# Attention scores in a two-block transformer kernel: the low part of the queries on 128 rows instead of 64

## Chip, cores and metric

One core of a Trainium2 chip. The metric is the device time of one execution in microseconds (us), median of the runs.

## What is computed

Two transformer layers (the first with retention, the second with neighbourhood attention over a grid of 512 latent tokens and 256 context tokens) and then one block with causal attention of 20 heads, a recurrent branch and gates. The change touches the two attentions, whose scores are products of queries and keys of 64 features per head. First the scores of layer 1 (16 heads, one row of the grid at a time, qr scaled by 1/8), then those of block 2 (12 dilated-window heads and 8 block heads over 512 tokens):

```
s_lat = jnp.einsum('bnqhd,brnkhd->bhnqrk', qr, kb).astype(jnp.float32) + bias[None].astype(jnp.float32)
s_lat = jnp.where(col_ok[:, :, None, :], s_lat, NEG_INF).reshape(B, NA_HEADS, n_cb, NA_QBLOCK_W, wr * NA_BAND_W)
s_ctx = jnp.einsum('bnqhd,bchd->bhnqc', qr, kc).astype(jnp.float32)
p = jax.nn.softmax(jnp.concatenate([s_lat, s_ctx], -1), -1).astype(v.dtype)
...
logits = jnp.einsum('bdhnqe,bdhnke->bdhnqk', qb, kk).astype(jnp.float32) * SCALE
logits = logits + bias[None, None, :, None]
...
lg = jnp.einsum('bhnqe,bhnke->bhnqk', qb, kb).astype(f32) * SCALE + bias_own[None, :, None]
```

## The kernel before, in words

All matrix products work on fp32r operands that are split in two: a rounded high part and the remainder, the low part, so that a product is high x high + high x low + low x high. ScalarE (ACT) writes the high part with a copy, VectorE (DVE) subtracts it from the source for the low part. Weights are loaded as slabs of 128 x 1024 (`Stream`, 384), split likewise, and live with nearly everything else in one pool of 86 tiles of 128 x 512 (`S`, 453).

The program is recorded first and then issued in the order of a list schedule (`Recorder.plan`, 152, and `issue`, 312): priority is program order, each instruction has a cost by its shape, and an instruction goes early if its engine is free and its tiles are. All instructions therefore carry line 321 in the profile, and are told apart by their tiles.

A pair of heads shares a projection. `na_proj` (1241, layer 1, 8 pairs) and `b2_proj` (1524, block 2, 10 pairs) multiply a weight slab with the activations (matmuls `bank<-act,w`), which leaves 128 x 512 in PSUM, head A on rows 0 to 63 and head B on rows 64 to 127. `q_stack` (1230) makes the queries: ACT copies each head's high part twice, onto both halves of a tile `qh` of its own; DVE subtracts once per head, and both low parts share one tile `ql`, A on rows 0 to 63, B on 64 to 127. `k_stack` (1237) makes a tile `kt` per head with the high part of the keys on one half of the rows and the low part on the other (`kc` for the context keys). So one matmul over 128 rows gives q high x (k high + k low), and a second over 64 rows adds q low x k high. Both are in `qk_mm` (1284), and follow each other in the same PSUM bank:

```
PE.matmul(out, H["q"][:, q0:q0 + 128], kt[:, c0:c1], start=True, stop=False)
PE.matmul(out, H["ql"][o:o + 64, q0:q0 + 128], kt[o:o + 64, c0:c1], start=False, stop=True)
```

In the profile the first is `bank<-kt,qh` or `bank<-kc,qh`, the second `bank<-kt,ql` or `bank<-kc,ql`. The queries are the stationary operand (128 columns), the keys the moving one (128, 256, 384 or 512 columns).

A head of layer 1 (`na_attn`, 1387) has 8 such pairs of matmuls (`na_scores`, 1301); DVE takes the maximum (tiles `mx`) and adds the bias (`s`), ACT takes exponentials, DVE divides (`na_soft`, 1325), PE transposes with the identity (`bank<-ident,sc`, `bank<-ident,s`), ACT and DVE split the result into high and low (`pt`, `na_trans`, 1340), PE multiplies with the values (`bank<-pt,vc`, `bank<-pt,vt`, `na_out`, 1370). The attention of pair p is interleaved with the projection of pair p + 1 (`interleave`, 426). A head of block 2 has 4 pairs (`Soft.scores`, in the class at 1548); `a_attn` (1633) takes three heads together, `c_attn` (1655) one at a time, again interleaved with projections. In the trace the first attention lies from 1384 to about 1672 us, the second from 2164 to about 2400.

Of the kernel before, what the change touches and what calls it, by code (L numbers as in the profile page):

```python
# [49 lines left out]


class Recorder:
    """Collects the program in program order, then issues it in the order of a list schedule.

    Priority is program order; a tile is taken ahead of program order only while every earlier
    instruction still finds its tiles free.
    """
    WINDOW = 2500
    SPARE, NEAR = 16, 200

# [89 lines left out]
        return n / (1.92 if fast else 0.96) + 69 + 60 * ptr, 0  # L150

    def plan(self):
        """List schedule of the program: its length, and when each instruction starts and ends."""
        ops = self.ops
        N = len(ops)
        prio = [op[7] for op in ops]
# [55 lines left out]
        while nd < N:  # L212
# [12 lines left out]
            while progressed:  # L225
                progressed = False
                for e in engs:
# [19 lines left out]
                    i = held  # L247
# [107 lines left out]


class Slab:
    """A [128, 1024] weight slab kept as two tiles."""

    def __init__(self, pool):  # L360
        self.t = [pool.tile([128, 512], F32R, name="w", tag="s", bufs=NSLOT) for _ in range(2)]
# [87 lines left out]
def body(nc, tc, io, sp, wp, pp, dp, order, stop=None, dbg=None):  # L449
# [3 lines left out]
    def S(dt=F32, name="s"):  # L453
        return sp.tile([128, 512], dt, name=name, tag="s", bufs=NSLOT)
# [71 lines left out]
            DVE.scalar_tensor_tensor(out if it == 2 else y, t, 1.5, y, op0=ALU.add, op1=ALU.mult)  # L526

    def mm3(out, a, b, start, stop):
        """a, b: (hi, lo) pairs of access patterns; a is stationary."""
        PE.matmul(out, a[0], b[0], start=start, stop=False)  # L530
        PE.matmul(out, a[0], b[1], start=False, stop=False)
        PE.matmul(out, a[1], b[0], start=False, stop=stop)

    # ---------------------------------------------------------------- constants
    kp = sp
    ident = kp.tile([128, 128], F32, name="ident", tag="ident", bufs=1)
    NCOL = io["cols"].shape[1] if order is not None else 1
# [19 lines left out]
    cond_bc = {}  # L557

    def ada_block(l, chunk, j, parts):
        """Shift or scale of features 128 j and up: products with the condition, summed along k on DVE."""  # L560
        for p in range(parts):
            if p not in cond_bc:
                cond_bc[p] = [S(name="cbc") for _ in range(2)]
                for g in range(2):
                    src = io["c_rows"][p:p + 1, g * 512:g * 512 + 512]
                    nc.sync.dma_start(cond_bc[p][g], src.to_broadcast([128, 512]))
                    ACT.activation(cond_bc[p][g], cond_bc[p][g], AF.Silu)
        w = [S(name="aw") for _ in range(2)]
        for g in range(2):
            nc.sync.dma_start(w[g], io["w_ada_t"][ADA_T.index((l, chunk)) * 8 + j][:, g * 512:g * 512 + 512])  # L570
        for p in range(parts):
            m = mcol[l][chunk][p][:, j:j + 1]
            for g in range(2):
                out = w[g] if p == parts - 1 else S(name="aj")
                init = m if g else col("ada_b", l * 48 + chunk * 8 + j)
                DVE.tensor_tensor_reduce(out, w[g], cond_bc[p][g], 1.0, init, ALU.mult, ALU.add, accum_out=m)

    def ada_pe(j):
        """Shift of layer 0, features 128 j and up, on PE."""
        b = bank()  # L580
        for k in range(8):
            if k % 4 == 0:
                w = S(name="ak")
                nc.sync.dma_start(w, io["w_ada_k"][j][:, k * 128:k * 128 + 512])
            PE.matmul(b[0:2, 0:128], cond[:, 2 * k:2 * k + 2], w[:, k % 4 * 128:k % 4 * 128 + 128],
                      start=(k == 0), stop=(k == 7))
        rows = S(name="rows")
        ACT.activation(rows[0:2, 0:128], b[0:2, 0:128], AF.Copy)
        PE.transpose(b[:, 256:258], rows[0:2, 0:128], ident[0:2, 0:2])
        for p in range(2):  # L590
            DVE.tensor_tensor(mcol[0][0][p][:, j:j + 1], b[:, 256 + p:257 + p], col("ada_b", j), op=ALU.add)
# [6 lines left out]
        ada_done.add((l, chunk))  # L598

    def ada_gate(l, chunk, parts):  # L600
        """A gate, token rows times features: sums over the partitions by ones on PE."""
        acc = {(p, g): None for p in range(parts) for g in range(2)}
        for g in range(2):
            for k in range(8):
# [27 lines left out]
    def ada_bg(l, chunk, parts):  # L632
        return (ada_gate if chunk in (2, 5) else ada_cols)(l, chunk, parts)

    # ------------------------------------------------------------ weights / GEMMs
    def out_banks(parts):
        return {p: bank() for p in parts}

    def t_mm(banks, w, act, ks, kts, cut=None, wk0=0):
        """T-form: out[128 features, tokens]; weights stationary."""  # L640
        h, l = w
        for k in ks:
            wa = (h[:, (k - wk0) * 128:(k - wk0) * 128 + 128], l[:, (k - wk0) * 128:(k - wk0) * 128 + 128])
            for pi, (wi, xi) in enumerate(((0, 0), (0, 1), (1, 0))):
                for p, b in banks.items():
                    c0, c1 = (0, 256 if p == "c" else 512) if cut is None else cut
                    PE.matmul(b[:, c0:c1], wa[wi], act.ap(k, xi, p, c0, c1),
                              start=(k == kts[0] and pi == 0), stop=(k == kts[-1] and pi == 2))
# [5 lines left out]
        return banks  # L654

    def t_gemm_first(keys, act, segs):
        """First slabs of a GEMM whose input arrives segment by segment."""
        wts = [ws.get(*k) for k in keys]
        parts = []
        for s in segs:  # L660
            if s[0] not in parts:
                parts.append(s[0])
        banks = [out_banks(parts) for _ in keys]
        for part, c0, c1, pre in segs:
            if pre is not None:
                pre()
            for b, w in zip(banks, wts):
                t_mm({part: b[part]}, w, act, range(8), range(8), (c0, c1))
                tick()
        return banks  # L670
# [4 lines left out]

    def r_sweep(name, base, nslab, act, tiles, k0=0, tail=0, on_tile=None, banks=None, fill=None, first=0,
                pre=None, width=512):
        """Row form: out[tokens, width]; activations stationary, 1024 // width k-tiles a slab."""
        banks = [bank() for _ in tiles] if banks is None else banks
        kps = 1024 // width  # L680

# [31 lines left out]
            ws.done(tail)  # L713
        return banks

    # ------------------------------------------------------------------ LN parts
    def add_gated(R, i, half, b, gate):
        if gate is None:
            DVE.tensor_tensor(R[i][half], b, R[i][half], op=ALU.add)
# [39 lines left out]
        return ap.rearrange("p (r n c) -> p n r c", r=8, n=4)  # L759

    def blocks(ap):
        """Grid columns of a [128, 512] tile kept column block by column block."""
        return ap.rearrange("p (n r c) -> p n r c", n=4, r=8)

    def to_T(rows, part, c0, act, G, Bc, grid=False):
        """rows: two token tiles (halves); writes act columns c0..c0+256 of `part`."""
        for kb in range(4):
            b = bank()
            for kk in range(2):
# [58 lines left out]
    TL0 = [("c", 0), ("c", 128)] + [("l", 128 * i) for i in range(4)]  # L828
    TL1 = [("l", 128 * i) for i in range(4)]

    # ================================================================= layer 0
    for ch in (2, 3, 4, 5):
        background.append(ada_bg(0, ch, 2))
    aT = Acts()
# [248 lines left out]
            ACT.activation(R[i][half], R[i][half], AF.Copy, scale=ALPHA)  # L1083

    def bound(sweep0, sweep1, R, tiles, gates, chain, segs_T, early=True):
        """Two half sweeps into rows; returns the hooks that finish the transposition.

        gates[i] is the gate of tile i; chain(i) runs once tile i is summed; segs_T(pair) transposes.
        """
        n = len(tiles)  # L1090
        banks = sweep0()
        for i in range(n):
# [110 lines left out]
    del uT, fT  # L1203
    dump("xn1", R[2][0])

    # ================================================================= layer 1
    ga, ba = bcast_row(io["ln_g"][1:2], ALPHA), bcast_row(io["ln_b"][1:2], ALPHA)
    h0d = dp.tile([512, 1024], F32, name="h0d", tag="h0d")

# [17 lines left out]

    HT = {}

    def q_stack(ps, scale, qa, qb, ql):  # L1230
        for q, p0 in ((qa, 0), (qb, 64)):
            for o in (0, 64):
                ACT.activation(q[o:o + 64], ps[p0:p0 + 64], AF.Copy, scale=scale)
            DVE.scalar_tensor_tensor(ql[p0:p0 + 64], ps[p0:p0 + 64], scale, q[p0:p0 + 64], op0=ALU.mult,
                                     op1=ALU.subtract)

    def k_stack(ps, p0, kt):
        ACT.activation(kt[p0:p0 + 64], ps[p0:p0 + 64], AF.Copy)
# [2 lines left out]
    def na_proj(p):  # L1241
# [4 lines left out]
            yield  # L1246
        A, B = {"o": 0}, {"o": 64}
        HT[2 * p], HT[2 * p + 1] = A, B
        A["q"], B["q"], ql = S(F32R, "qh"), S(F32R, "qh"), S(F32R, "ql")
        A["ql"] = B["ql"] = ql  # L1250
        q_stack(b["l"], 0.125, A["q"], B["q"], ql)
        ws.done()
        raw, rawc = S(name="vr"), S(name="vr")
        nc.sync.dma_start(raw.rearrange("p (t c) -> p t c", t=4),
# [27 lines left out]
        yield  # L1282

    def qk_mm(out, H, q0, kt, c0, c1):
        o = H["o"]
        PE.matmul(out, H["q"][:, q0:q0 + 128], kt[:, c0:c1], start=True, stop=False)
        PE.matmul(out, H["ql"][o:o + 64, q0:q0 + 128], kt[o:o + 64, c0:c1], start=False, stop=True)

    KB = ((0, 2), (0, 3), (1, 4), (2, 4))

# [164 lines left out]
    X = {}  # L1455

    def chain_h(i):
        """h = LN(z) rows, kept for the residual; X = h / rms(h)."""
        mv, rstd = ln_rstd(i)
        for half in range(2):  # L1460
            DVE.scalar_tensor_tensor(R[i][half], R[i][half], mv[:, 0:1], ga[half], op0=ALU.subtract, op1=ALU.mult)
# [13 lines left out]
    del uT, fT  # L1475
    dump("h1", R[0][0])

    # ================================================================= block 2
    h1d = dp.tile([4, 2, 128, 512], F32, name="h1d", tag="h1d")
    for i in range(4):  # L1480
        for half in range(2):
# [42 lines left out]
    def b2_proj(qn, kn, t, heads):  # L1524
# [4 lines left out]
            yield  # L1529
        A, B = {"o": 0}, {"o": 64}  # L1530
        HT[heads[0]], HT[heads[1]] = A, B
        A["q"], B["q"], ql = S(F32R, "qh"), S(F32R, "qh"), S(F32R, "ql")
        A["ql"] = B["ql"] = ql
        q_stack(b["l"], 0.125, A["q"], B["q"], ql)
        ws.done()
        w = ws.get(kn, t)
        b = out_banks("l")
# [8 lines left out]
        yield  # L1546

    class Soft:
        """Causal attention of one output head over one or more groups of keys."""

        def __init__(self, heads, st):
            self.heads, self.st = heads, st
# [122 lines left out]
    def chain(*gs):  # L1675
        for g in gs:
            yield from g
# [345 lines left out]
```

## Time and profile before

| what | value |
|---|---|
| median of 3 runs | 3029.85 us |
| lowest and highest | 3027.33 and 3034.6 us |
| profiled execution, span from first to last instruction | 3022.2 us |
| its own time with what lies around the span | not listed; the median is 7.65 us above the span |
| granted TensorE clock, mean over the span | 0.981 of 2.4 GHz |
| busy share PE, DVE, ACT, POOL | 97%, 54%, 37%, 23% |

The page gives shares over the whole span, the views of the trace give single stretches. Matmuls are pipelined: the next starts before the one ahead ends, so the duration of one is longer than its place in the queue, and a row of the timeline with xN runs from the first start to the last end. PEld is the load of a stationary tile.

### The profile page before, as it was taken

Reading aid. Unit: us, or ns where it says so; the run is one execution under the profiler, and the core shown is the slowest. Engines: PE = TensorE matmul, PEld = TensorE weight load, DVE = VectorE, ACT = ScalarE, POOL = GpSimd, SP = SyncE. Lnnn points to the kernel's source line nnn. Section 1 sums busy time; section 2 is a strip of 40 time slices with the busy share of each in tenths; the row PEclk is TensorE's granted clock in tenths of the full one; section 3 lists DMA queues with packets and bytes.
Section 4 is the critical chain, followed back from the end, with each engine's and each line's share of the span. In section 5 each row is a group of like instructions: output and inputs, shape, how many; then the busy total and the mean of one; then the engine's idle time right before and its main releaser. Section 6 shows DMA issues by size and latency. Waiting matters only on the chain.

```text
span 3022.2 us, 37734 instructions
## 1 busy us (share of the span) xinstructions
PE 2943.5 (97%) x13988; PEld 2418.1 (80%) x13988; DVE 1640.3 (54%) x3351; ACT 1105.1 (37%) x2343; POOL 706.0 (23%) x592
## 2 busy tenths in 40 slices
PE   7999999998999999999999899998999999999998
PEld 5788888887888888877777788886777778888887
DVE  8887544428735344554777932337365673553233
ACT  4332333512221222224656432323465653332231
POOL 4311213106212112251221521104333201121100
PEclk9999999999999999998999999998999999999999
DMA  8333212322324333231212332334422222332231
GB/s 312 112 129 108 91 51 82 119 94 87 117 75 163 102 108 133 89 130 56 70 63 84 106 105 70 100 110 155 149 84 84 70 84 91 119 102 80 77 112 42
DMA packets 120462, 311.01 MB, mean 103 GB/s; under 512 B 12646, under 2 KB 22230, under 8 KB 120278
## 3 DMA queue, kind: packets, MB, share of 16 engines
q1 hardware_dynamic: 120278, 308.60, 31.0%
q8 instruction: 110, 1.80, 0.2%
q14 instruction: 74, 0.61, 0.1%
HBM read 292.77 MB, written 22.33 MB: 104 GB/s over the span
## 4 chain that ended last, share of the span: by engine, by line
PE 90%; DVE 6%; DMA 2%; ACT 1%; issue 1%; POOL 1%; SPq 0%; DVEq 0%; ACTq 0%; POOLq 0%
PE bank L321 90%; DVE rs_t L321 1%; DVE R L321 1%; DVE w L321 1%; DVE rs_g L321 1%; DVE act L321 1%; DMA ak<-w_ada_k 0%; DMA xl<-xT 0%; DVE bn L321 0%; DVE gt L321 0%; DMA aw<-w_ada 0%; DVE rstd L321 0%; ACT w L321 0%; DMA cbc<-c_rows 0%; DVE X L321 0%
## 5 line engine op out<-in xcount | busy, mean ns | idle before, releaser
L321 PE MATMUL bank<-act,w 128*128 128x512 f32 (+1 forms) x6960 | 1452.6, 367 | 11.3 <-ACT act L321 6.5
L321 PEld LDWEIGHTS bank<-act,w 128*128 128x128 f32 x6960 | 1186.6, 191 | 233.0 <-issue 9.6
L321 DVE TENSOR_TENSOR w<-raw,w 128x512 fp32r<-128x512 f32 x664 | 524.2, 812 | 546.0 <-PE bank L321 333.0
L321 ACT ACTIVATE w<-raw 128x512 fp32r<-128x512 f32 x748 | 440.2, 628 | 516.9 <-PE bank L321 362.9
L321 PE MATMUL bank<-w,act 128*128 128x512 f32 (+1 forms) x1728 | 391.8, 387 | 4.3 <-DVE w L321 3.3
L321 PEld LDWEIGHTS bank<-w,act 128*128 128x128 f32 x1728 | 320.1, 190 | 70.4 <-DVE w L321 4.4
L321 PE MATMUL bank<-w,f 128*128 128x512 f32 x1584 | 365.0, 390 | 0.0
L321 PEld LDWEIGHTS bank<-w,f 128*128 128x128 f32 x1584 | 297.4, 188 | 61.4
L321 POOL TENSOR_TENSOR f<-sg,f 128x512 fp32r<-128x512 f32 x66 | 86.7, 1313 | 520.3 <-ACT f L321 505.5
L321 POOL TENSOR_TENSOR R<-gt,R 128x512 f32<-128x512 f32 x64 | 88.1, 1397 | 383.5 <-DVE gt L321 369.7
L321 POOL TENSOR_TENSOR w<-raw,w 128x512 fp32r<-128x512 f32 x84 | 111.1, 1349 | 203.7 <-ACT w L321 180.3
L321 PE MATMUL bank<-w,yT 128*128 128x512 f32 x576 | 133.5, 393 | 0.0
L321 PEld LDWEIGHTS bank<-w,yT 128*128 128x128 f32 x576 | 108.6, 189 | 22.5
L321 ACT ACTIVATE f<-sg 128x512 fp32r<-128x512 f32 x66 | 41.7, 632 | 202.0 <-DVE sg L321 201.9
L321 ACT ACTIVATE pt<-bank 128x384 fp32r<-128x384 f32 (+3 forms) x176 | 72.7, 470 | 100.9 <-PE bank L321 100.2
L321 DVE TENSOR_TENSOR pt<-bank,pt 128x384 fp32r<-128x384 f32 (+3 forms) x176 | 84.4, 522 | 45.7 <-ACT pt L321 42.7
L321 DVE TENSOR_TENSOR sg<-bank,sg 128x512 f32<-128x512 f32 x66 | 45.4, 688 | 109.1 <-PE bank L321 109.1
L321 POOL TENSOR_TENSOR act<-tt,act 128x256 fp32r<-128x256 f32 (+1 forms) x88 | 77.5, 908 | 80.2 <-DVE act L321 71.7
L321 ACT ACTIVATE s<-s,nm 128x384 f32<-128x384 f32 (+3 forms) x144 | 79.5, 559 | 35.4 <-DVE nm L321 35.4
L321 POOL TENSOR_TENSOR R<-R,bc 128x512 f32<-128x512 f32 x56 | 81.2, 1464 | 15.2 <-PE bank L321 13.4
L321 DVE TENSOR_TENSOR gt<-bank,gbc 128x512 f32<-128x512 f32 x64 | 42.9, 685 | 76.4 <-PE bank L321 71.5
L321 DVE SCALAR_TENSOR_TENSOR acc<-aw,cond,acc 128x512 f32<-128x512 f32 x84 | 67.6, 830 | 27.0 <-DMA aw<-w_ada 26.4
(217 smaller groups left out, 3079.4 us busy)
## 6 DMA issues: line engine op xcount, KB each, us to landing
raw<-w_w SPq DMA_DIRECT2D x132, 512.0 KB, 3.5
aw<-w_ada_t SPq DMA_DIRECT2D x112, 256.0 KB, 4.4
raw<-w_b_gu SPq DMA_DIRECT2D x44, 512.0 KB, 3.5
aw<-w_ada SPq DMA_DIRECT2D x64, 256.0 KB, 5.1
raw<-w_b_gt SPq DMA_DIRECT2D x24, 512.0 KB, 3.5
raw<-w_b_dn SPq DMA_DIRECT2D x22, 512.0 KB, 3.6
raw<-w_ret_qk SPq DMA_DIRECT2D x16, 512.0 KB, 3.5
raw<-w_ret_v SPq DMA_DIRECT2D x16, 512.0 KB, 4.7
```

What stands on the lines that cost most here:

```text
L321: ins = fn(*a, **k).ins
```

## The change

`q_stack` now makes a `qh` and a `ql` of its own for each head, and writes the low part onto both halves of the tile, with two subtractions per head where there was one. `qk_mm` multiplies the whole 128 rows of `ql` with the whole 128 rows of `kt`, so that the second matmul also has 128 rows; it now adds q low x (k high + k low). The low x low part was not computed before. A few texts between triple quotes and comments are gone too.

```
-    def q_stack(ps, scale, qa, qb, ql):
-        for q, p0 in ((qa, 0), (qb, 64)):
+    def q_stack(ps, scale, A, B):
+
+        for H, p0 in ((A, 0), (B, 64)):
+            q, ql = H["q"], H["ql"] = S(F32R, "qh"), S(F32R, "ql")
             for o in (0, 64):
                 ACT.activation(q[o:o + 64], ps[p0:p0 + 64], AF.Copy, scale=scale)
-            DVE.scalar_tensor_tensor(ql[p0:p0 + 64], ps[p0:p0 + 64], scale, q[p0:p0 + 64], op0=ALU.mult,
-                                     op1=ALU.subtract)
+            for o in (0, 64):
+                DVE.scalar_tensor_tensor(ql[o:o + 64], ps[p0:p0 + 64], scale, q[p0:p0 + 64], op0=ALU.mult,
+                                         op1=ALU.subtract)
...
-        A["q"], B["q"], ql = S(F32R, "qh"), S(F32R, "qh"), S(F32R, "ql")
-        A["ql"] = B["ql"] = ql
-        q_stack(b["l"], 0.125, A["q"], B["q"], ql)
+        q_stack(b["l"], 0.125, A, B)
...
     def qk_mm(out, H, q0, kt, c0, c1):
-        o = H["o"]
         PE.matmul(out, H["q"][:, q0:q0 + 128], kt[:, c0:c1], start=True, stop=False)
-        PE.matmul(out, H["ql"][o:o + 64, q0:q0 + 128], kt[o:o + 64, c0:c1], start=False, stop=True)
+        PE.matmul(out, H["ql"][:, q0:q0 + 128], kt[:, c0:c1], start=False, stop=True)
```

The lines in the middle stand alike in `na_proj` and `b2_proj`. The new subtractions and tiles go through the list schedule, so the order of all engines shifts from the first attention on. Three places in it (the shapes in these rows are those of the output; before is shown first, then the change).

DVE in the first attention, where the probabilities of head 4 (`pt`) are split and the queries of heads 6 and 7 (`ql`) are made; `nm` is the maximum of head 5, `w` a weight slab.

```order
L321 TENSOR_SCALAR nm<-nm 128x4
L321 SCALAR_TENSOR_TENSOR ql<-bank,qh 64x512
L321 TENSOR_TENSOR pt<-bank,pt 128x256
L321 TENSOR_TENSOR w<-raw,w 128x512
L321 TENSOR_TENSOR pt<-bank,pt 128x512 x2
L321 TENSOR_TENSOR pt<-bank,pt 128x384 x2
L321 TENSOR_TENSOR pt<-bank,pt 128x256
L321 TENSOR_TENSOR w<-raw,w 128x512
```

```order
L321 ISA nm 128x1
L321 SCALAR_TENSOR_TENSOR ql<-bank,qh 64x512
L321 TENSOR_SCALAR nm<-nm 128x4
L321 TENSOR_TENSOR pt<-bank,pt 128x512
L321 SCALAR_TENSOR_TENSOR ql<-bank,qh 64x512
L321 TENSOR_TENSOR pt<-bank,pt 128x512
L321 TENSOR_TENSOR pt<-bank,pt 128x256
L321 TENSOR_TENSOR pt<-bank,pt 128x384
L321 TENSOR_TENSOR w<-raw,w 128x512
L321 TENSOR_TENSOR pt<-bank,pt 128x384
```

One subtraction stood ahead of the splits of `pt` before, and the pair's other one 24 rows earlier; now one stands ahead of them and one between them, and the pair's other two 17 and 24 rows earlier.

PE in the first attention, the transposes of head 4 (`bank<-ident,sc` and `bank<-ident,s`) among the projection of heads 6 and 7 (`bank<-act,w`).

```order
L321 MATMUL bank<-ident,sc 128x128 x6
L321 MATMUL bank<-act,w 128x256
L321 MATMUL bank<-ident,sc 128x128 x2
L321 MATMUL bank<-act,w 128x512
L321 MATMUL bank<-act,w 128x256
L321 MATMUL bank<-ident,s 128x128 x2
L321 MATMUL bank<-act,w 128x512
L321 MATMUL bank<-act,w 128x256
L321 MATMUL bank<-ident,s 128x128 x3
L321 MATMUL bank<-act,w 128x512
```

```order
L321 MATMUL bank<-ident,sc 128x128 x3
L321 MATMUL bank<-act,w 128x256
L321 MATMUL bank<-act,w 128x512
L321 MATMUL bank<-act,w 128x256
L321 MATMUL bank<-act,w 128x512
L321 MATMUL bank<-ident,sc 128x128
L321 MATMUL bank<-act,w 128x256
L321 MATMUL bank<-act,w 128x512
L321 MATMUL bank<-ident,sc 128x128 x4
L321 MATMUL bank<-ident,s 128x128 x2
L321 MATMUL bank<-act,w 128x256
```

The first eight transposes have one projection matmul among them before, and six now.

DVE in the second attention, where the first three heads are split (`pt`) and the next pair's queries are made (`ql`); `rd` is the reciprocal of the softmax sum.

```order
L321 TENSOR_SCALAR s<-s,rd_3985 128x512
L321 SCALAR_TENSOR_TENSOR ql<-bank,qh 64x512
L321 TENSOR_TENSOR pt<-bank,pt 128x512
L321 TENSOR_TENSOR pt<-bank,pt 128x384
L321 TENSOR_TENSOR pt<-bank,pt 128x256
L321 TENSOR_TENSOR pt<-bank,pt 128x128
```

```order
L321 TENSOR_SCALAR s<-s,rd_3996 128x512
L321 SCALAR_TENSOR_TENSOR ql<-bank,qh 64x512 x2
L321 TENSOR_TENSOR pt<-bank,pt 128x512
L321 SCALAR_TENSOR_TENSOR ql<-bank,qh 64x512
L321 TENSOR_TENSOR pt<-bank,pt 128x384
L321 TENSOR_TENSOR pt<-bank,pt 128x256
L321 TENSOR_TENSOR pt<-bank,pt 128x128
```

Where one subtraction stood ahead of the splits of `pt`, two stand now, and a further one between the splits.

## Rows read from the trace of the kernel before

**Rows 1.** The page, part 1: busy time, share of the span and instructions of the engines.

```profile
PE 2943.5 (97%) x13988; PEld 2418.1 (80%) x13988; DVE 1640.3 (54%) x3351; ACT 1105.1 (37%) x2343; POOL 706.0 (23%) x592
```

**Rows 2.** The page, part 4: the chain that ended last, its shares of the span by engine.

```profile
PE 90%; DVE 6%; DMA 2%; ACT 1%; issue 1%; POOL 1%; SPq 0%; DVEq 0%; ACTq 0%; POOLq 0%
```

**Rows 3.** PE groups by line and shape: names, shapes, count; busy us, mean ns; idle before.

```profile
L321 PE MATMUL bank<-kc,ql 64*128 64x256 f32 x64 | 25.0, 391 | 0.0
L321 PE MATMUL bank<-kc,qh 128*128 128x256 f32 x64 | 23.4, 365 | 0.0
```

**Rows 4.** Timeline of PE, first burst of scores: start us, duration us, what, count.

```profile
1384.37 0.38 PE L321 MATMUL bank<-kc,qh 128*128 128x256 f32 x1
1384.68 0.38 PE L321 MATMUL bank<-kc,ql 64*128 64x256 f32 x1
```

**Rows 5.** Timeline of PE, a burst of the second attention.

```profile
2164.54 0.28 PE L321 MATMUL bank<-kt,qh 128*128 128x256 f32 x1
2164.74 0.38 PE L321 MATMUL bank<-kt,ql 64*128 64x256 f32 x1
2165.05 0.33 PE L321 MATMUL bank<-kt,qh 128*128 128x128 f32 x1
2165.31 0.32 PE L321 MATMUL bank<-kt,ql 64*128 64x128 f32 x1
2165.57 0.44 PE L321 MATMUL bank<-kt,qh 128*128 128x384 f32 x1
2165.93 0.44 PE L321 MATMUL bank<-kt,ql 64*128 64x384 f32 x1
2166.30 0.50 PE L321 MATMUL bank<-kt,qh 128*128 128x512 f32 x1
2166.74 0.50 PE L321 MATMUL bank<-kt,ql 64*128 64x512 f32 x1
2167.17 1.66 PE L321 MATMUL bank<-act,w 128*128 128x512 f32 x6
```

**Rows 6.** Timeline of PE, two unbroken runs of 128-row matmuls and what follows each.

```profile
722.31 5.91 PE L321 MATMUL bank<-act,w 128*128 128x256 f32 x48
728.06 0.60 PE L321 MATMUL bank<-ident,R 128*128 128x128 f32 x4
...
1672.29 20.38 PE L321 MATMUL bank<-w,oT 128*128 128x512 f32 x89
1692.50 0.60 PE L321 MATMUL bank<-ident,R 128*128 128x128 f32 x4
```

**Rows 7.** Both attentions: us, busy PE, PEld, DVE, ACT, POOL (count); PEclk, DMA share, GB/s.

```profile
1384.00:1672.00 288.00, 287.37 (x1313) 220.38 (x1312) 215.82 (x535) 180.12 (x505) 53.52 (x68) 0.91 0.21 67
2160.00:2400.00 240.00, 238.91 (x1106) 183.00 (x1105) 137.83 (x400) 143.44 (x362) 63.13 (x49) 1.00 0.23 74
```

**Rows 8.** Waits of DVE, 1384 to 1672 us: total us, times, longest.

```profile
DVE pt L321 <- ACT pt L321: 37.5, 31, 6.6
DVE mx L321 <- PE bank L321: 9.9, 14, 3.3
DVE s L321 <- PE bank L321: 7.1, 15, 0.8
```

**Rows 9.** Waits of ACT, 1384 to 1672 us.

```profile
ACT pt L321 <- PE bank L321: 90.2, 29, 7.5
```

**Rows 10.** Tile ql: count, ns min/median/max, first and last start us, forms.

```profile
L321 PE MATMUL bank<-kt,ql x144: 322/409/686, 1386.6 to 2393.7; 64*128 64x384 f32 x52, 64*128 64x256 f32 x52, 64*128 64x128 f32 x20, 64*128 64x512 f32 x20
L321 PE MATMUL bank<-kc,ql x64: 378/382/579, 1384.1 to 1645.3; 64*128 64x256 f32 x64
L321 DVE SCALAR_TENSOR_TENSOR ql<-bank,qh x36: 651/689/696, 1375.7 to 2332.5; 64x512 fp32r<-64x512 f32 x36
```

**Rows 11.** Around the first burst of scores, columns as in rows 7.

```profile
1383.00:1389.00 6.00, 6.00 (x22) 3.48 (x20) 4.54 (x10) 1.84 (x5) 1.69 (x2) 1.00 0.01 3
1389.00:1393.00 4.00, 4.00 (x11) 2.70 (x10) 1.03 (x4) 0.00 (x0) 0.00 (x0) 0.57 0.01 2
```

More of the change, by code (lines that the diff above doesn't have):

```diff
@@ L1531, in b2_proj @@
         HT[heads[0]], HT[heads[1]] = A, B
-        A["q"], B["q"], ql = S(F32R, "qh"), S(F32R, "qh"), S(F32R, "ql")
-        A["ql"] = B["ql"] = ql
-        q_stack(b["l"], 0.125, A["q"], B["q"], ql)
+        q_stack(b["l"], 0.125, A, B)
         ws.done()
```

## The prediction

> **What bounds the kernel now.** I read the page first: TensorE (PE) is busy 97% of the span [rows 1] and carries 90% of the chain that ended last [rows 2]. So an edit that shortens PE's work pays, until another engine takes its place. Then the groups by line and shape for the two kinds of score matmul: a high-part matmul (stationary qh, 128 rows) lasts 365 ns on average, a low-part one (stationary ql, 64 rows) 391 ns [rows 3]. Read by durations, the 64-row shape costs next to nothing more. But these matmuls are pipelined, so what counts is the time from one start to the next, and that stands in the timeline. Where the shapes alternate, a 256-column matmul moves the next start 0.31 us on, high part (1384.37 to 1384.68) or low part (2164.74 to 2165.05) alike [rows 4, 5]; 48 of the same width among 128-row neighbours take 728.06 - 722.31 = 5.75 us, 0.12 each, with another stationary tile loaded for each as well [rows 6]. The 89 of 512 columns take 20.21 us, 0.227 each [rows 6], against 0.44 and 0.43 in alternation [rows 5]. So each change of row count costs about 0.2 us that no group of durations and no wait shows: PE counts as busy through it.
>
> The Trainium skill, "TensorE: Matmul & The Clock Gate", section "Why this matters for your kernels", says that a matmul with a small contraction takes the same time as a full one; a lone shape may do so, and the durations here nearly agree, but the steps between mixed shapes do not. By that rule the sum below would be 0 instead of 78 us for PE.
>
> Last I split the time by stage. The first attention (1384 to 1672 us) has PE busy 287.4 of 288 us, VectorE (DVE) 215.8, ScalarE (ACT) 180.1; the second (2160 to 2400 us) 238.9, 137.8 and 143.4 of 240 [rows 7].
>
> **Part 1, the score matmuls become one shape.** The counts stand beside ql: 64 with the context keys and 144 with the others, together 116 of 256 columns, 52 of 384, 20 of 512 and 20 of 128, and as many high ones beside them [rows 10]. A pair of them now takes, and will take at 128-row steps:
> - 256: 0.31 + 0.31, then 2 x 0.12: saves 0.38 us.
> - 384: 0.36 + 0.37 [rows 5], then 2 x 0.17 (an estimate halfway between 0.12 and 0.227): saves 0.39.
> - 512: 0.44 + 0.43, then 2 x 0.227: saves 0.42.
> - 128: 0.26 + 0.26 [rows 5], then at most 2 x 0.12: saves 0.28.
>
> The first attention has 96 pairs of 256 and 32 of 384: 36.5 + 12.5 = 49.0 us. The second has 20 of each width: 20 x 1.47 = 29.4 us. Together 78.4 us of PE time. A burst taken whole agrees: the eight matmuls from 2164.54 to 2167.17 take 2.63 us where 2 x (0.12 + 0.12 + 0.17 + 0.227) = 1.27 would do; 1.36 of the 1.47, the rest being the step after the burst.
>
> **Part 2, the added subtractions.** Each of the 18 head pairs issues four low-part subtractions on DVE instead of two: 36 more of 0.689 us [rows 10], 24.8 us of DVE time. In the first attention 14 of these lie inside the stage (the first pair's stand ahead of it): 9.6 us; in the second 20: 13.8 us. Nobody waits for DVE there today; what hides them is DVE's idle time, 288 - 215.8 = 72.2 us and 240 - 137.8 = 102.2 us. They stand in the queue ahead of the evacuations of transposed probabilities (the order rows), so those come up to 1.4 us later per pair. No DMA and no wait on a queue is added; the sixteen copies and the loads only shift places.
>
> **Part 3, the extra tile.** A second ql per pair takes one more of the 86 slots of the shared pool for as long as its head lives. No place in the trace shows PE short of a slot in these stages: I cost it at nothing, and at a few us if weight splits come late; the order moves weight loads by a row or two only.
>
> **What it is worth by stage.** First attention: PE alone would need 287.4 - 49.0 = 238.4 us. DVE needs 215.8 + 9.6 = 225.4 us of work plus the idle time that does not come from a late PE. Of the 72.2 us idle, 37.5 + 9.9 + 7.1 = 54.5 us are waits for pt, mx and s [rows 8], the first of them behind ACT copies that themselves waited 90.2 us for PE [rows 9]; I let the other 17.7 us stay. So DVE's floor is 225.4 + 17.7 = 243.1 us, above PE's: in this stage **DVE becomes the bound**, and not all of the 49 us is kept. I take 248 us, a tenth of the 54.5 us staying: 40 us saved. The ends: if all idle vanished, 225.4 us, 62.6 saved; if half of the 54.5 stayed, 270 us, 18 saved.
>
> The granted clock falls in this stage: 1.00 over the first burst (1383 to 1389 us) and 0.57 in the four us behind it [rows 11], that is mostly the lower of its two levels, 1.2 GHz; over the stage the mean is 0.91 [rows 7], so at most 0.09 x 288 = 26 us of PE time lies there. In the second attention, where the bursts are as mixed but thinner, it stays at 1.00. Part of the 26 us may come back, but only below DVE's floor, so I count it at 0; it matters for the low end alone.
>
> Second attention: with 29.4 us less, DVE would be busy 151.6 of some 211 us and ACT 143.4, so PE stays the bound. I deduct 1.4 us, two subtractions of 0.689 for a pair whose scores follow soon: 28 us saved (ends 22 and 29.4).
>
> Sum: 40 + 28 = 68 us. The profiled execution spans 3022.2 us and would come to 2954. Its time outside the span isn't listed; the median of the runs, 3029.85, lies 7.65 us above the span, and I let that stand: 3029.85 - 68 = **2962 us**.
>
> **The rivals.**
> - DVE gives up nearly all its idle time and the clock holds (B): 62.6 + 29.4 = 92 us, 2938. For it: the waits of rows 8 are nearly all late PE. Against it: in-order queues seldom run gapless.
> - DVE locks in (C): the added subtractions delay the evacuations, PE now waits for transposed tiles, and half of the 54.5 us stays: 18 + 22 = 40 us, 2990. For it: DVE is at 75% already, and the transposes are now spread among more projection matmuls (the order rows). Against it: the projections that fill PE's queue are independent of the chain.
> - The change does not do what it says (D): the 0.2 us belongs to the swap of stationary tiles or to two matmuls accumulating in one bank, not to the row count. Then PE keeps its steps, the subtractions hide, and it stays at 3030. Against it: the 48 matmuls of 0.12 us also swap their tiles and accumulate [rows 6], and the high part at 2164.54, which comes from 128-row work, has a step of 0.20 us [rows 5], beside 0.31 for one that comes from a 64-row matmul [rows 4]. The Trainium skill, "TensorE: Matmul & The Clock Gate", section "The mechanism", says a weight load overlaps a running matmul only where the row groups differ. By that rule full-height matmuls would gain nothing; rows 6 speak against it.
> - Slower (E): DVE's idle time is latency of ACT, not slack behind PE. Then DVE sets both stages, its idle stays as it is and each added subtraction lengthens the time: 36 x 0.689 = 24.8 us, up to 3055. It decides once less of DVE's idle goes than the subtractions add: 9.6 of 72.2 us and 13.8 of 102.2 us. Against it: the 90.2 us that ACT waited for PE [rows 9].
>
> **How the numbers follow.** Measurement of this kernel tells about 0.2% from no change, 6 us. Forecast, 2948 to 2976: 0.57. B, 2936 to 2948: 0.14. C, 2976 to 2992: 0.18. D: 0.06. E: 0.05, a fifth of it too small to be told from no change. The range 2936 to 2990 leaves out D, E and the edge of C, less than 2 in 10. Faster 0.89, same 0.07, slower 0.04.
>
> **What would show it.** Right: low-part matmuls of 128 rows, 256-column steps near 0.12 in bursts; PE's busy time down by 60 to 80 us in the two stages; 72 subtractions instead of 36; the first attention near 248 us with DVE busy over 90% and PE now waiting for DVE or ACT; the second near 212 us with PE still full. Wrong: steps still near 0.3 (D), a first attention near 270 us (C) or near 225 (B), or a later stage that grew because its weight splits came late.

## The result and the profile after

The changed kernel takes 2953.68 us (median of 4 runs, 2952.65 to 2955.22) against 3032.22 us of the kernel before (4 runs, 3027.33 to 3038.32): ratio 0.9749, 95% interval 0.9732 to 0.9765, faster by 78.5 us at the medians. The profiled execution spans 2952.1 us, 70.1 less than before, and its own time is 2953.83 us.

The timeline of PE, the first burst of the second attention, answers to [rows 5]:

```profile
2119.98 0.28 PE L321 MATMUL bank<-kt,qh 128*128 128x256 f32 x1
2120.09 0.28 PE L321 MATMUL bank<-kt,ql 128*128 128x256 f32 x1
2120.21 0.22 PE L321 MATMUL bank<-kt,qh 128*128 128x128 f32 x1
2120.28 0.28 PE L321 MATMUL bank<-kt,ql 128*128 128x128 f32 x1
2120.39 0.39 PE L321 MATMUL bank<-kt,qh 128*128 128x384 f32 x1
2120.62 0.34 PE L321 MATMUL bank<-kt,ql 128*128 128x384 f32 x1
2120.79 0.40 PE L321 MATMUL bank<-kt,qh 128*128 128x512 f32 x1
2121.02 0.39 PE L321 MATMUL bank<-kt,ql 128*128 128x512 f32 x1
2121.26 1.52 PE L321 MATMUL bank<-act,w 128*128 128x512 f32 x6
```

All shapes are 128 rows now, and the eight score matmuls take 2121.26 - 2119.98 = 1.28 us where the burst of before took 2.63. The 256-column steps are 0.11 and 0.12 us (2119.98 to 2120.21), the 128-column ones 0.07 and 0.11, the 384-column ones 0.23 and 0.17, the 512-column ones 0.23 and 0.24. The view of tile ql, as [rows 10]:

```profile
L321 PE MATMUL bank<-kt,ql x144: 272/331/442, 1384.7 to 2323.9; 128*128 128x384 f32 x52, 128*128 128x256 f32 x52, 128*128 128x128 f32 x20, 128*128 128x512 f32 x20
L321 DVE SCALAR_TENSOR_TENSOR ql<-bank,qh x72: 669/688/696, 1375.1 to 2272.7; 64x512 fp32r<-64x512 f32 x72
L321 PE MATMUL bank<-kc,ql x64: 277/282/287, 1383.4 to 1606.1; 128*128 128x256 f32 x64
```

72 subtractions of the same duration as before, and the low part of 256 columns with the context keys lasts a median of 282 ns instead of 382. PE's busy time fell with it, by the page's part 1 from 2943.5 us to this:

```profile
PE 2858.1 (97%) x13988; PEld 2383.1 (81%) x13988; DVE 1669.6 (57%) x3387; ACT 1106.3 (37%) x2343; POOL 701.4 (24%) x592
```

Both attentions, from the first score matmul to the last product with the values (columns as in [rows 7]):

```profile
1383.30:1629.40 246.10, 232.48 (x1319) 191.21 (x1318) 229.69 (x551) 182.09 (x506) 50.03 (x67) 0.99 0.25 81
2120.00:2337.10 217.10, 213.99 (x1127) 181.04 (x1126) 151.69 (x429) 148.84 (x374) 63.63 (x49) 1.00 0.27 85
```

The first attention lasts 246.1 us instead of 288 and the second 217.1 instead of 242.7, by this row of the kernel before:

```profile
2164.50:2407.20 242.70, 241.62 (x1127) 185.51 (x1127) 142.57 (x414) 148.26 (x373) 61.85 (x48) 1.00 0.24 75
```

The first begins 0.7 us earlier, the stretch between them is 490.6 us (1629.4 to 2120.0) instead of 492.5, and the rest of the span did not move. So 41.9 + 25.6 + 0.7 + 1.9 = 70.1 us (the ends of the first attention of before were taken in whole microseconds, so some 0.3 us may stand in a neighbouring term). DVE is busy 229.7 of 246.1 us, 93% instead of 75%. PE, whose only waits in the first attention of before were these two (1384 to 1672 us; us in total, times, longest), now has gaps:

```profile
PE bank L321 <- DVE nm L321: 0.4, 1, 0.4
PE bank L321 <- DVE pt L321: 0.2, 1, 0.2
```

The longest waits of PE, some of DVE and the longest of ACT in the changed kernel, 1383 to 1628 us (the last two answer to [rows 8, 9]):

```profile
PE bank L321 <- DVE sc L321: 5.8, 12, 0.8
PE bank L321 <- DVE nm L321: 3.9, 8, 0.9
PE bank L321 <- DVE pt L321: 1.4, 8, 0.3
```

```profile
DVE oT L321 <- ACT ot L321: 5.6, 6, 1.4
DVE pt L321 <- ACT pt L321: 0.9, 2, 0.5
DVE mx L321 <- PE bank L321: 0.7, 1, 0.7
```

```profile
ACT pt L321 <- PE bank L321: 46.3, 35, 4.6
```

DVE hardly waits for scores or transposes any more (37.5, 9.9 and 7.1 us before, 0.9, 0.7 and none now), and PE waits 11.1 us for DVE's quotients (sc), maxima (nm) and splits (pt). The bound has passed from PE to DVE only in part: PE is still busy 232.5 of the 246.1 us, 94%, as full as DVE with its 93%. The clock behind the first burst, as [rows 11]:

```profile
1383.00:1386.00 3.00, 2.92 (x20) 2.59 (x20) 2.22 (x4) 1.29 (x4) 0.74 (x1) 1.00 0.00 0
1386.00:1390.00 4.00, 4.00 (x26) 3.65 (x25) 3.97 (x14) 0.45 (x1) 0.00 (x0) 1.00 0.02 6
```

It stays at 1.00, the higher level of 2.4 GHz, where it fell to 0.57 before; over the stage the mean is 0.99 instead of 0.91.

The runs of the kernel before spread over 17 us, and with the clock. In the 17 runs beside the first experiments, 3022.3 us goes with a mean granted clock of 0.982 and 3039.02 us with 0.974. The changed kernel's four runs lie within 2.6 us. The profile of before shows one of the faster executions, which is why the spans differ by 70.1 us and the medians by 78.5.

### The profile page after: what moved, and what is told of

Same layout as the page of the kernel before. It is cut to its first block, busy times and chain, and to the rows that moved or that the text cites. A ratio compares the mean times of both kernels' runs of the same rounds, so it can differ in the third digit from the quotient of the medians.

```text
span 2952.1 us, 37759 instructions
## 1 busy us (share of the span) xinstructions
PE 2858.1 (97%) x13988; PEld 2383.1 (81%) x13988; DVE 1669.6 (57%) x3387; ACT 1106.3 (37%) x2343; POOL 701.4 (24%) x592
## 4 chain that ended last, share of the span: by engine, by line
PE 41%; DVE 7%; ACT 2%; issue 1%; POOL 0%; DMA 0%; DVEq 0%; ACTq 0%; POOLq 0%
PE bank L321 41%; DVE s L321 2%; ACT s L321 1%; DVE pt L321 1%; DVE rs_t L321 1%; DVE R L321 0%; DVE mx L321 0%; DVE ql L321 0%; DVE act L321 0%; DVE sc L321 0%; DVE w L321 0%; DVE rs_g L321 0%; DVE X L321 0%; DVE lruc L321 0%; DVE kt L321 0%
## 5 line engine op out<-in xcount | busy, mean ns | idle before, releaser
L321 PE MATMUL bank<-act,w 128*128 128x512 f32 (+1 forms) x6960 | 1430.8, 364 | 9.4 <-ACT act L321 6.8
L321 POOL TENSOR_TENSOR act<-tt,act 128x256 fp32r<-128x256 f32 (+1 forms) x88 | 77.1, 904 | 78.5 <-DVE act L321 70.3
L321 ACT ACTIVATE pt<-bank 128x512 fp32r<-128x512 f32 (+3 forms) x176 | 72.8, 468 | 54.9 <-PE bank L321 54.2
```

The source lines that it names most:

```text
L321: ins = fn(*a, **k).ins
```

## Experiments

Nine kernels, each timed beside the kernel before: e1 to e7 on one chip, e8 and e9 on another. The ratios compare with the runs of before in the same session, whose medians went from 3028.2 to 3032.22 us. The changed kernel's runs are of the first session alone, so a difference from it of up to some 4 us in the median settles nothing by itself. The stage columns are those of the windows view, from the first score matmul to the last product with the values, in one profiled execution each.

| kernel | median us | ratio to before, 95% | first attention: length, DVE busy, DVE idle | second: length |
|---|---|---|---|---|
| before | 3032.22 | 1 | 288, 215.8, 72.2 | 242.7 |
| changed | 2953.68 | 0.9749, 0.9732 to 0.9765 | 246.1, 229.7, 16.4 | 217.1 |
| e1, subtractions only | 3039.5 | 1.0035, 1.0022 to 1.0048 | 306.1, 226.3, 79.8 | 244.4 |
| e2, shape only | 2943.76 | 0.9715, 0.9694 to 0.9736 | 235.8, 216.8, 19.0 | 215.6 |
| e3, lows grouped | 2957.5 | 0.9758, 0.9738 to 0.9779 | 242.0, 217.4, 24.6 | 222.9 |
| e4, copy on ACT | 2948.75 | 0.9730, 0.9709 to 0.9750 | 241.3, 218.6, 22.7 | 214.5 |
| e5, copy on POOL | 2946.91 | 0.9723, 0.9704 to 0.9742 | 236.8, 213.7, 23.1 | 216.2 |
| e6, splits on POOL | 2946.26 | 0.9722, 0.9704 to 0.9741 | 239.3, 214.1, 25.2 | 216.9 |
| e7, ACT copy and POOL splits | 2940.97 | 0.9706, 0.9687 to 0.9724 | 242.4, 206.5, 35.9 | 214.8 |
| e8, subtractions doubled | 2980.86 | 0.9847, 0.9829 to 0.9864 | 252.4, 242.6, 9.8 | 234.2 |
| e9, POOL copy and POOL splits | 2942.4 | 0.9717, 0.9702 to 0.9733 | 228.8, 198.7, 30.1 | 216.2 |

**e1, the subtractions alone.** The low-part matmul of the changed kernel goes back to 64 rows:

```
-        PE.matmul(out, H["ql"][:, q0:q0 + 128], kt[:, c0:c1], start=False, stop=True)
+        o = H["o"]
+        PE.matmul(out, H["ql"][o:o + 64, q0:q0 + 128], kt[o:o + 64, c0:c1], start=False, stop=True)
```

> The changed kernel's queries (a low tile per head, four subtractions per pair), but the low-part matmul keeps its 64 rows as before. Theory (the gain comes from the row count of the matmuls alone, and the added subtractions hide in DVE's idle time as long as PE is late): no gain, 256-column steps stay near 0.31 us, time within 6 us of the kernel before, the first attention stays near 288 us. Rival (DVE's idle time is latency, so that each added subtraction lengthens the time): up to 24.8 us slower. Rival (the gain came from the new order or the separate tiles): faster by tens of us.

It is 11 us slower than the kernel before (3028.2 us in the runs beside it), where at most 6 were expected. The windows of both attentions, and the wait of DVE that grew:

```profile
1383.70:1689.80 306.10, 303.25 (x1320) 228.25 (x1319) 226.25 (x551) 180.95 (x506) 53.20 (x67) 0.87 0.20 65
2178.80:2423.20 244.40, 242.48 (x1127) 185.80 (x1126) 153.34 (x429) 148.73 (x374) 63.00 (x49) 1.00 0.23 76
```

```profile
DVE pt L321 <- ACT pt L321: 51.2, 27, 6.6
```

So the tiles and the order of the change bring nothing, and the whole gain needs the row count. But the subtractions are not free either. The rival's mechanism is not what the rows show: DVE's idle grew from 72.2 to 79.8 us, the wait for pt from 37.5 to 51.2, while PE is busy 303.3 of 306.1 us. PE still sets this stage, and it runs at a mean clock of 0.87 instead of 0.91. In this profile more of the stage's matmuls fell into stretches at the lower level. But over the runs the mean clock, 0.975 to 0.979, overlaps with that of the kernel before, and at the same mean clock e1 is still the longer: at 0.979 its four runs take 3038.93 to 3040.01 us, the five of before (over all sessions) 3024.44 to 3027.38. So the mean clock of the span does not account for the 11 us, and their cause stays open.

**e2, the shape alone.** The kernel before, with its shared low tile, and only this:

```
-        o = H["o"]
...
-        PE.matmul(out, H["ql"][o:o + 64, q0:q0 + 128], kt[o:o + 64, c0:c1], start=False, stop=True)
+        PE.matmul(out, H["ql"][:, q0:q0 + 128], kt[:, c0:c1], start=False, stop=True)
```

> The kernel before with one edit: the low-part matmul takes all 128 rows of the shared low tile and of the keys. It thereby adds the other head's low queries times the wrong half of the keys, so its scores are not the reference's; no subtraction is added. Theory (128-row steps; in the first attention DVE then sets the time): steps 0.12 us, the second attention 25 to 28 us shorter, the first about 215.8 us of DVE work plus the 16.7 us of idle that the changed kernel shows, 232 to 237 us instead of 245, so 8 to 12 us faster than the changed kernel, 78 to 90 below the kernel before. Rival (PE still sets the first attention of the changed kernel, the subtractions cost nothing): as the changed kernel, 70 to 78 us below the kernel before.

2943.76 us, 9.9 us below the changed kernel and as the theory gave. Its windows:

```profile
1386.70:1622.50 235.80, 227.05 (x1315) 189.51 (x1314) 216.84 (x535) 182.06 (x505) 51.98 (x68) 1.00 0.25 82
2114.40:2330.00 215.60, 213.62 (x1128) 180.76 (x1126) 141.92 (x414) 148.35 (x373) 62.02 (x48) 1.00 0.26 85
```

The first attention is 10.3 us shorter than in the changed kernel, with 12.9 us less DVE work; the second 1.5 us. DVE is still busy 92% of the stage, PE 96%. So the added subtractions, with the second tile and the order that come with them, cost the changed kernel about 10 us, nearly all of it in the first attention.

**e3, low parts grouped.** The kernel before, 64-row low parts; each head issues its high parts first:

```
-    def qk_mm(out, H, q0, kt, c0, c1):
+    def qk_all(H, jobs):
         o = H["o"]
...
+        names = [j[0].tensor.name for j in jobs] if order is not None else [0] * len(jobs)
+        for i, (out, q0, kt, c0, c1) in enumerate(jobs):
+            PE.matmul(out, H["q"][:, q0:q0 + 128], kt[:, c0:c1], start=names[i] not in names[:i], stop=False)
+        for i, (out, q0, kt, c0, c1) in enumerate(jobs):
+            PE.matmul(out, H["ql"][o:o + 64, q0:q0 + 128], kt[o:o + 64, c0:c1], start=False,
+                      stop=names[i] not in names[i + 1:])
...
```

Both callers now collect the jobs of a head and call `qk_all` once.

> The kernel before, 64-row low parts and one shared low tile, but all high-part matmuls of a head are issued first and then all low parts, so that the row count changes 2 to 4 times per head instead of 16 (first attention) or 8 (second). Theory (the price stands at each change of the row count, in both directions): steps between two 64-row matmuls of 256 columns as short as between 128-row ones, 0.12 us, and 0.2 us only at the changes; the first attention then near DVE's floor of 232 to 240 us, the second 20 to 24 us shorter, together 65 to 80 us below the kernel before. Rival (a 64-row matmul is dear by itself): its steps stay near 0.3 us, only the high parts gain, 39 of 78 us of PE time, 30 to 40 us below the kernel before.

2957.5 us, 4 above the changed kernel with not one 128-row low part, and 71 below the kernel before in the runs beside it. The timeline of PE, the start of each attention (a row with xN carries the shape of its first matmul; the x4 rows hold several widths):

```profile
1384.15 0.63 PE L321 MATMUL bank<-kc,qh 128*128 128x256 f32 x4
1384.71 0.62 PE L321 MATMUL bank<-kc,ql 64*128 64x256 f32 x3
1385.26 0.85 PE L321 MATMUL bank<-kt,qh 128*128 128x384 f32 x4
...
2117.78 0.80 PE L321 MATMUL bank<-kt,qh 128*128 128x256 f32 x4
2118.51 0.90 PE L321 MATMUL bank<-kt,ql 64*128 64x256 f32 x4
2119.34 1.66 PE L321 MATMUL bank<-act,w 128*128 128x512 f32 x6
```

Three 64-row matmuls of 256 columns take 1385.26 - 1384.71 = 0.55 us, with part of the price of the change at either end; inside, from the second start to the third (1384.94 to 1385.06 in the trace), the step is 0.12 us, as between 128-row ones. In the second attention the eight matmuls of a head take 2119.34 - 2117.78 = 1.56 us: 2.63 in the kernel before, 1.28 in the changed one. So a 64-row matmul is not dear by itself; the change of row count is, in both directions, and the number of changes sets the price. The windows show the same, with the clock at 0.99 and 1.00:

```profile
1384.20:1626.20 242.00, 232.85 (x1308) 190.39 (x1307) 217.41 (x536) 181.81 (x506) 51.14 (x68) 0.99 0.25 82
2117.80:2340.70 222.90, 221.70 (x1129) 179.12 (x1128) 141.12 (x414) 148.94 (x374) 62.15 (x48) 1.00 0.25 82
```

The first attention comes out just above the 232 to 240 us expected, the second 19.8 us shorter than before where 20 to 24 were expected. Counted over PE's rows in the traces, the row count changes 160 times in the second attention of the kernel before, 42 times in e3's and never in e2's; these last 242.7, 222.9 and 215.6 us, all at a clock of 1.00 and with the same subtractions. That is 0.17 us for each change, from 160 to none as from 42 to none. In the first attention it changes 246, 54 and 0 times, and there the clock differs as well.

**e4 and e5, the second half copied.** The changed kernel; one subtraction per head on DVE, and a copy of the low part to the other half on ACT (e4) or POOL (e5):

```
-            for o in (0, 64):
-                DVE.scalar_tensor_tensor(ql[o:o + 64], ps[p0:p0 + 64], scale, q[p0:p0 + 64], op0=ALU.mult,
-                                         op1=ALU.subtract)
+            DVE.scalar_tensor_tensor(ql[p0:p0 + 64], ps[p0:p0 + 64], scale, q[p0:p0 + 64], op0=ALU.mult,
+                                     op1=ALU.subtract)
+            ACT.activation(ql[64 - p0:128 - p0], ql[p0:p0 + 64], AF.Copy)
```

e5 has `POOL.tensor_copy(ql[64 - p0:128 - p0], ql[p0:p0 + 64])` in the last line's place.

> The changed kernel, but the second half of each low tile is copied by ACT from the first half instead of being subtracted again by DVE: 36 subtractions of 0.689 us less on DVE, 36 copies of about 0.59 us more on ACT. Theory (DVE sets the first attention): DVE sheds 9.6 us there and the stage shrinks by 5 to 9 us; the second attention, where PE sets the time, stays as it is or loses 1 to 2 us to a longer chain. Rival (PE's and ACT's chain sets the stage, DVE is only busy beside it): no change, or slower by up to 10 us because ACT's copies for the probabilities come later.

> The changed kernel, but the second half of each low tile is copied by POOL from the first half: 36 subtractions less on DVE, nothing more on ACT. Theory (DVE sets the first attention): as with the copy on ACT, the stage 5 to 10 us shorter than in the changed kernel, 5 to 10 us below it in all. Rival (POOL's copy is slow and late, and PE waits for the low tile): no gain or up to 5 us slower than the changed kernel.

4.9 and 6.8 us below the changed kernel; neither's runs (at most 2950.39 and 2947.9) reach its lowest, 2952.65. Their first attentions, e4's row and then e5's:

```profile
1387.10:1628.40 241.30, 230.35 (x1320) 190.42 (x1318) 218.59 (x537) 191.74 (x519) 50.02 (x67) 1.00 0.25 82
```

```profile
1386.00:1622.80 236.80, 227.18 (x1312) 188.91 (x1311) 213.66 (x537) 180.74 (x505) 60.86 (x81) 1.00 0.26 84
```

DVE sheds 11 and 16 us, the stage 4.8 and 9.3, where 5 to 9 and 5 to 10 were expected; the second attention, where e4 was to gain nothing, fell by 2.6 and 0.9. Of what DVE sheds, the 14 subtractions are 9.6 us in both; the rest lies in other groups, whose durations differ from kernel to kernel (`sc<-sc,dl` has a mean of 428 ns in the changed kernel and 402 in e5) for a reason that no run shows. Whether the copy costs more on ACT (191.7 us busy instead of 182.1) than on POOL is not settled: e5's stage is the shorter by 4.5 us, but the totals differ by 1.8 us with overlapping runs.

**e6, e7 and e9, weight splits off DVE.** The changed kernel with this around the first attention (e6), together with the copy on ACT (e7) and on POOL (e9):

```
     na_v(1)
+    ws.lo = POOL
     drain(na_proj(0))
...
+    ws.lo = None
     del aT
     na_trans(15)
```

> The changed kernel with the weight splits of the first attention moved from DVE to POOL (36 of 0.74 us there, 26 us of DVE work; POOL is busy 50 of 245 us). Theory (DVE sets the stage at 228 us of work plus 17 us of idle): the stage falls towards PE's own 212 us, to 220 to 232 us, 13 to 25 us below the changed kernel in all. Rival (the stage is set by the chain of a head through PE, ACT and DVE, not by DVE's load): DVE gets idle time and the stage stays within 5 us of 245.

> Both: the second half of each low tile copied by ACT and the weight splits of the first attention on POOL. Theory: DVE's work falls to about 193 us in the first attention, below PE's 212 us, so PE sets the stage: 215 to 228 us, 18 to 30 us below the changed kernel in all, and no further gain from unloading DVE. Rival (the chain of a head sets the stage): as the copy on ACT alone, 5 us below the changed kernel.

> The changed kernel with the second half of each low tile copied by POOL and the weight splits of the first attention on POOL too. If the chain of a head through PE, ACT and DVE is what remains after DVE is unloaded: the first attention stays at 236 to 243 us although DVE's work falls to about 205 us; in all 2938 to 2945 us, as with the copy on ACT. If DVE's load still counted: 225 to 230 us and 2927 to 2933 us in all.

Their first attentions, in this order, and between them the group of splits on POOL in e6:

```profile
1384.30:1623.60 239.30, 229.79 (x1335) 193.39 (x1334) 214.07 (x528) 182.56 (x507) 82.91 (x95) 1.00 0.26 84
```

```profile
L321 POOL TENSOR_TENSOR w<-raw,w 128x512 fp32r<-128x512 f32 x25 | 32.1, 1303 | 31.1 <-ACT w L321 25.2 <-PE bank L321 6.0
```

```profile
1383.10:1625.50 242.40, 233.11 (x1341) 193.88 (x1340) 206.47 (x515) 192.07 (x521) 82.90 (x95) 1.00 0.25 83
```

```profile
1383.70:1612.50 228.80, 220.82 (x1299) 186.46 (x1298) 198.65 (x507) 179.84 (x501) 92.80 (x109) 1.00 0.24 81
```

25 splits went over to POOL, not 36. Against the changed kernel e6 gains 7.4 us, e7 12.7 and e9 11.3, but the first attention does not follow DVE's load: with 206.5 us of DVE work it lasts 242.4 us (e7), with 214.1 it lasts 239.3 (e6), with 198.7 it lasts 228.8 (e9). DVE's idle time grows as its work falls. In e7 the stage shrank by 3.7 us only, and 7 us came from the stretch between the attentions, 483.4 us instead of 490.6. So the numbers expected for the stage of e6 and e7, on the ground that DVE alone sets it, did not come. e9's did in the stage (225 to 230 us) and not in the total (2927 to 2933 us); 4.3 us of the gain went behind the stage, with 494.9 us between the attentions. Below some 214 us of DVE work neither DVE nor PE is full there (85% and 96% in e7), and each waits in turn for the other; each kernel is also issued in an order of its own. How much of the stage then follows DVE's load stays open.

**e8, the subtractions doubled.** Each is issued twice:

```
-            for o in (0, 64):
+            for o in (0, 64, 0, 64):
                 DVE.scalar_tensor_tensor(ql[o:o + 64], ps[p0:p0 + 64], scale, q[p0:p0 + 64], op0=ALU.mult,
                                          op1=ALU.subtract)
```

> The changed kernel with every low-part subtraction issued twice (the second writes the same values again): 72 more of 0.689 us on DVE, 28 of them, 19.2 us, inside the first attention. Theory (from the changed kernel's load upward DVE's work sets the first attention one for one): the stage grows by 15 to 20 us to 261 to 266 us, the second attention by 0 to 5 us, in all 16 to 24 us above the changed kernel. Rival (the chain of a head sets the stage at about 240 us and DVE's load counts only in part, as it seems below the changed kernel's load): 5 to 12 us in all.

27 us above the changed kernel, more than either expected, and in another place. Both attentions and PE's wait for ql in the second:

```profile
1385.80:1638.20 252.40, 230.92 (x1309) 189.38 (x1308) 242.56 (x578) 180.70 (x506) 53.22 (x67) 0.99 0.24 78
2129.50:2363.70 234.20, 222.28 (x1127) 186.65 (x1125) 175.61 (x462) 147.71 (x372) 60.73 (x47) 0.96 0.24 78
```

```profile
PE bank L321 <- DVE ql L321: 7.3, 4, 2.7
```

The first attention grew by 6.3 us for 12.9 us of DVE work, not one for one but by half, as the rival has it. The 28 more subtractions there are 19.2 us as expected; DVE's busy time grew by less because its other groups came out 6.3 us shorter (`s<-s,dl` with a mean of 453 ns instead of 497). The second grew by 17.1 us: PE waits 7.3 us for low tiles there, 1.7 in the changed kernel (the last rows below), and the clock, 1.00 in the changed kernel, comes to 0.96. PE's gaps grew by 8.8 us of these (217.1 - 214.0 to 234.2 - 222.3) and its busy time by 8.3.

```profile
PE bank L321 <- DVE ql L321: 1.7, 2, 1.2
PE bank L321 <- DVE s L321: 0.6, 1, 0.6
PE bank L321 <- DVE mx L321: 0.3, 1, 0.3
PE bank L321 <- DVE pt L321: 0.2, 1, 0.2
```

## Why the prediction was right

- **The step between shapes.** The burst of 1.27 us came out at 1.28. Within it the 128-column steps were 0.06 us shorter than counted and the 384-column ones 0.06 longer, which cancels by luck; the 256- and 512-column ones were right to 0.02. That durations hide this and starts show it was the reading that mattered. e3 shows the price to stand at the change of row count, as part 1 had it, with 0.17 us in the length of the stage for the 0.2 read from the steps. On the Trainium skill's rule that a small contraction takes as long as a full matmul ("TensorE: Matmul & The Clock Gate", section "Why this matters for your kernels"): e3's runs of 64-row matmuls bear it out among their own kind at 256 columns (a step of 0.12 us), and beside 128-row ones it fails (0.31).
- **DVE becomes the bound of the first attention.** 246.1 us against 248 forecast, in part by luck: its work came to 229.7 us instead of 225.4 and its idle time to 16.4 instead of 22.6, errors of 4.3 and 6.2 us that nearly cancel. The added subtractions were 9.6 us as counted; the 4.3 lie in other groups, in `s<-s,dl` above all, whose 64 instructions lasted 497 ns on the mean instead of 436. The count of which waits would go (rows 8) held almost exactly: 37.5 us of waiting for pt became 0.9. But DVE is not the bound alone. PE is as full, and over the changed kernel, e2 and e4 to e9 the stage goes up by about half a microsecond for each of DVE's: 228.8 at 198.7, 252.4 at 242.6, and e7 off the line at 242.4.
- **PE's time and the clock in the first attention.** PE's busy time fell by 54.9 us (287.4 to 232.5) where 49.0 were counted, and the mean clock rose from 0.91 to 0.99. The 26 us of the clock, counted at 0, came back at least in part: e2 and e9 last 235.8 and 228.8 us, below the 238.4 that PE alone was to need at the old clock. No run separates what of the changed kernel's 41.9 us there is the clock's.
- **The added subtractions.** "What hides them is DVE's idle time" was wrong as a sentence: with their tile and order they cost 9.9 us (e2), and e1, which has them without the new shape, is 11 us slower on a path that stays open. The sum did carry them, as 9.6 us in DVE's floor, so the total didn't suffer.
- **The second attention.** 28 us was forecast, 25.6 came (242.7 to 217.1). The mis-sized term is mostly PE's 29.4 us: without the added subtractions e2 gains 27.1, as 20 bursts of 1.35 us would (2.63 to 1.28), where the four widths were added up to 1.47. The 1.4 us deducted for the later low tiles was right: the changed kernel stands 1.5 us above e2, and PE has 2.8 us of waits there, 1.7 of them for ql.
- **Outside the two stages** 2.6 us more went, which the sum did not have.
- **From span to median.** The forecast of 2962 (2961.85 before rounding) is 8.2 us above the median. Of these, 2.1 are in the sum (2954.2 forecast for the span, 2952.1 found). The other 6.1 are the step in which the 7.65 us between span and median was let stand: the changed kernel's median is 1.6 us above its span. Time outside the span is 1.7 us in the changed kernel's profiled run (2953.83 us) and 1.8 us in a later run of the kernel before (3022.3 us, span 3020.5). The rest was that the profiled execution of before was a fast one by its clock. The clock came in here too: by the way the runs of before go with it, their median had paid more of it than the profile showed.
- **The rivals.** B needed DVE's idle time to vanish; 16 us stayed. C needed half of the waiting to stay. D is refuted by the steps and by e3. The Trainium skill's rule beside it ("TensorE: Matmul & The Clock Gate", section "The mechanism"), that loads overlap only across row groups, would have given full-height matmuls nothing, and they gained 1.35 us per burst; the same section also lets a load into a background weight buffer go ahead, which no run here tells apart. E is refuted for the changed kernel, which gained; e8 shows that it is not far: with twice the added subtractions, PE waits for low tiles and the clock falls.

e7 is the fastest of all these kernels, 2940.97 us against 2953.68, its interval wholly below the changed kernel's; e9 is level with it, and the difference between the two was not settled.

## What to carry to other kernels

Read a pipelined engine by the distance of its starts, not by the durations of its instructions: matmuls of different row counts lasted almost the same and cost 0.17 to 0.2 us at each change, with PE counted as busy. Before costing the gain in full, subtract what the next engine needs in the same stretch; here DVE's work plus the idle time that was not PE's fault gave the stage to 2 us, with two larger errors that cancelled. And where an edit can sort instructions by shape (e3), most of such a price is to be had without any added work.

## What was not expected of the hardware

- Matmuls of 64 rows pay where they border on 128-row ones, on both sides, but run among themselves as fast as these where the trace has them side by side at 256 columns (a step of 0.12 us). A burst takes 1.56 us grouped, 1.28 all on 128 rows, 2.63 alternating.
- In the first attention the granted clock goes with the alternation: 0.91 on the mean with it, 0.99 to 1.00 in the changed kernel and in e2 to e9, though PE is busy less there, 91% to 97% instead of 99.8%. That alternation is the cause is not shown: the second attention stays at 1.00 with 160 changes of row count.
- The lower level comes without alternation too, where PE has gaps. In the changed kernel, between the attentions, the row below has PE busy 33.1 of 47 us and a mean clock of 0.82 (columns as in [rows 7]; but for two matmuls of 36 rows all there have 128). In e8's second attention, where PE waits for low tiles and is busy 222.3 of 234.2 us, the mean is 0.96.

```profile
2025.00:2072.00 47.00, 33.12 (x165) 28.10 (x164) 46.17 (x117) 20.53 (x51) 31.93 (x29) 0.82 0.65 237
```
